# Every fourth weight tile's low part from an accumulating DMA instead of a VectorE subtraction

## The chip, the cores and the metric

One NeuronCore of a Trainium2 chip runs the whole program in one launch. The metric is device time in microseconds, the median of several runs. TensorE (PE in the profile, with PEld for its weight loads) makes the matrix products, VectorE (DVE), ScalarE (ACT) and GpSimd (POOL) work elementwise, and SyncE (SP) issues loads from memory. GpSimd and ScalarE can issue DMAs too. All DMAs run on the same sixteen DMA engines.

## What is computed

Two transformer blocks over 256 tokens of width 2048, batch 1, in float32. Cut to what matters here:

```python
def first_block(x, meta_tokens, ...):          # 16 meta tokens go ahead of the 256
    proj = rmsnorm(h, norm1_w) @ w_in            # 2048 x 4112
    ...                                          # gated linear attention, causal pooling
    h = h + mixed @ w_out                        # 2048 x 2048
    z = rmsnorm(h, norm2_w) @ mlp_w1             # 2048 x 8192
    h = h + jnp.square(jax.nn.relu(z)) @ mlp_w2  # 8192 x 2048
    return rmsnorm(h, final_norm_w)[:, N_META:]

def second_block(x, mem, ...):
    x = layer_norm(ALPHA * x + hybrid_mixer(x, ...), ...)            # w_in 2048 x 9552, w_out
    x = layer_norm(ALPHA * x + mem_cross_attention(x, mem, ...), ...)
    x = layer_norm(ALPHA * x + swiglu(x, w_ffn_in, w_ffn_out), ...)  # 2048 x 11264, 5632 x 2048
    return x
```

What costs time is the products of 256 (or 272) activations with some 450 MB of float32 weights, each of which is used once.

## The kernel before

**Weights as two parts.** TensorE multiplies in float32r, a rounded float32. To keep the accuracy each operand x is held as hi + lo: hi is x rounded to float32r, lo is x - hi. A product is then the sum of three: hi by hi, hi by lo and lo by hi. Activations are split where they are made; weights are split tile by tile as they come in.

**The stream of tiles.** All weights lie in memory in the order of use, cut into 870 tiles of mostly 128 partitions x 1024 float32 (512 KB; two blocks of 128 rows, 512 columns). The class `Stream` holds them. For tile s, `fill` issues the load from SP into a buffer `wraw` (line 51; three buffers, `RAW`), then on ScalarE the rounding copy to `whi` (line 63) and on VectorE the subtraction `wlo = wraw - whi` (line 64; four buffers each, `SPLIT`). `fill` is called by `next`, each time that the program takes a tile for its products. It issues the split of tiles up to two ahead of the one that is taken, and loads up to three ahead of the split. So `whi` and `wlo` of tile s take the buffers of tile s - 4, and `wraw` the buffer of an earlier tile whose split is done. Each engine runs its instructions in the order in which the program issued them, and waits by semaphores for those of other engines.

**The products.** A `TJob` makes out[feature, token] with the weights stationary: for each of four column blocks and two row blocks, a product of `wlo` with the activations' hi part (line 256, 256 columns) and one of `whi` with both parts (line 257, 512 columns). An `NJob` makes out[token, feature] with the activations stationary: three products a step (lines 273 to 275; 274 reads `wlo`). PSUM has six banks `acc` for these. Between products, `side.pump()` issues other work in small steps: evacuations, norms, attention. Of that, some goes to GpSimd: the power function of the norms (`power`, line 377), half of the LayerNorm's scaling in `Turn.prep` (line 469), and DMA loads of row vectors and of the memory tokens (`load`, line 183).

**Order.** The schedule is manual: the order of the program text is the order on each engine. Only the buffer that a new tile gets is chosen for it: of a tag's buffers the pool gives the one that it reckons free first.

Of the kernel before, what the change touches and what calls it, by code (L numbers as in the profile page):

```python
# [11 lines left out]
F32 = mybir.dt.float32  # L12
F32R = mybir.dt.float32r
I32 = mybir.dt.int32
AF = mybir.ActivationFunctionType
# [17 lines left out]
class Stream:  # L33
    """Weight tiles in the order in which the products use them: loaded ahead, and split
    into two float32r parts (hi + lo == w exactly)."""
# [7 lines left out]
    def fill(self, ahead=LOOK):  # L43
        n = len(self.specs)
        nc = self.nc
        while True:
# [11 lines left out]
            if self.s < min(n, self.i + min(ahead, 1 + self.i // 5), self.d):  # L58
# [5 lines left out]
                nc.vector.tensor_tensor(lo, t, hi.bitcast(F32), op=OP.subtract)  # L64
# [21 lines left out]
class Side:  # L86
    """Work that is issued in small pieces between the products of the main sequence.
    Lanes 0 and 1 have a PSUM bank each; lane 2 is for work that needs none."""
# [11 lines left out]
    def post(self, gen):  # L100
        """A chain of steps on one result; one step at a time, chains in order."""
        if isinstance(gen, GeneratorType) and next(gen, self) is not self:
            self.posts.append(gen)
# [38 lines left out]
def wtile(name, kbs, pieces):  # L142
    """One weight tile: rows of the blocks kbs (consecutive), columns of pieces."""
# [9 lines left out]
def hybrid_two_block_kernel(ctx: ExitStack, tc: tile.TileContext, a, out):  # L153
# [40 lines left out]
    def early(d):  # L194
        """Loads between those of the first weights."""
# [23 lines left out]
    prog = []  # L219

    class TJob:
        """out[feature, token]: weights stationary. blocks: (first column, width) in the tile."""
# [39 lines left out]
    class NJob:  # L262
        """out[token, feature]: activations stationary, weights moving."""
# [13 lines left out]
        def run(self):  # L277
# [23 lines left out]
            # the last steps, of one group: the first token tile as a whole before the second  # L301
# [16 lines left out]
    class Call:  # L318
        """fn at this place of the sequence; what is pending is issued first."""
# [31 lines left out]
    def join(dst, b, scale=None, rb=None):  # L351
        """dst = scale * (both halves of the bank) * rb, in two steps"""
# [34 lines left out]
    def square_scale(st, eps, name):  # L387
        """Per token 1 / (mean square + eps), along the partitions."""
# [12 lines left out]
    def row_scale(get, name, parts=((0, 128), (128, 128))):  # L401
        """Per token 1 / rms, along the partitions and along the free axis in all partitions.
        get: the mean square + eps of a part."""
# [19 lines left out]
    def turn_raw(XT, i, g):  # L423
        """Rows of the residual times a weight per feature to XT[feature, block, hi/lo, token]."""
# [16 lines left out]
    class Turn:  # L441
        """LayerNorm of the residual, in place without ln_g and ln_b, and with both to XT."""
# [49 lines left out]
        def spread(self):  # L492
            """As side work."""
# [369 lines left out]
    XT = {}  # L863
# [793 lines left out]
```

## Time and profile before

| | |
|---|---|
| median of 3 runs | 2547.06 us (2547.0 to 2547.12) |
| span of the profiled execution | 2543.4 us |
| TensorE busy | 2520.1 us, 99% |
| VectorE busy | 1611.4 us, 63% |
| ScalarE busy | 1190.8 us, 47% |
| GpSimd busy | 60.6 us, 2% |
| weight tiles | 870, one per 2.92 us of the span |
| DMA | 472.93 MB, mean 186 GB/s |

The profile is one execution; its span runs from the first instruction to the last. Busy time counts an engine's instructions, without waits and without the issuing of DMAs. A group of instructions is named by line, engine, operation and out<-in with the buffers' names; "idle before" is the time in which its engine stood still just ahead of these instructions, and the name behind it is what ended most of that.

### The profile page before, as it was taken

To read this page: it belongs to the slowest core of one execution; us is meant where nothing else is said; L and a number is where in the kernel's file an instruction comes from. 1 tells how busy PE (TensorE), PEld (TensorE's weight loads), DVE (VectorE), ACT (ScalarE), POOL (GpSimd) and SP (SyncE) were. 2 spreads that over 40 slices of the span, in tenths; PEclk is the share of its full clock that TensorE was granted. 3 is DMA by queue.
4 is the path that set the end of the run, shared out by engine and by line. 5 is a ranking of instruction groups with operands and counts; after the bars stand their busy time and mean duration, and the time that the engine had idled before them with its cause. 6 is when DMAs were issued, how large, how long until landed. Compare 5 with 4: busy or idle time off the path is not lost.

```text
span 2543.4 us, 34921 instructions
## 1 busy us (share of the span) xinstructions
PE 2520.1 (99%) x13581; PEld 2160.9 (85%) x13581; DVE 1611.4 (63%) x2240; ACT 1190.8 (47%) x1680; POOL 60.6 (2%) x82
## 2 busy tenths in 40 slices
PE   8999999999999999999999999999999999999998
PEld 8897888888888888888888888888788888888886
DVE  5655666556656656768656667767775555565557
ACT  5444444444444444444544565555544444444443
POOL 0000000000000000000000000020200000000000
PEclk9999999999999999999999999999999999999999
DMA  8444555555566565555555555665566666566664
GB/s 278 133 160 147 164 190 189 191 191 191 183 198 197 190 193 190 187 168 181 172 174 166 166 185 188 224 218 165 190 190 190 193 189 195 186 197 189 193 193 156
DMA packets 132326, 472.93 MB, mean 186 GB/s; under 512 B 14992, under 2 KB 16352, under 8 KB 131888
## 3 DMA queue, kind: packets, MB, share of 16 engines
q1 hardware_dynamic: 128624, 460.77, 56.5%
q0 software_dynamic: 3104, 9.32, 1.3%
q8 instruction: 106, 1.74, 0.3%
q10 hardware_dynamic: 432, 0.61, 0.1%
q14 instruction: 60, 0.49, 0.1%
HBM read 468.54 MB, written 2.10 MB: 185 GB/s over the span
## 4 chain that ended last, share of the span: by engine, by line
PE 96%; DVE 2%; DMA 1%; ACT 1%; issue 0%; POOL 0%; SPq 0%; DVEq 0%; ACTq 0%; POOLq 0%
PE acc L257 34%; PE acc L256 17%; PE acc L273 11%; PE acc L274 11%; PE acc L275 11%; PE acc L253 2%; PE acc L247 2%; PE acc L249 2%; PE acc L248 2%; DMA wraw<-in_weights_dram 1%; PE acc L254 1%; DVE wlo L64 1%; PE aux L1160 0%; PE aux L1090 0%; ACT whi L63 0%
## 5 line engine op out<-in xcount | busy, mean ns | idle before, releaser
L64 DVE TENSOR_TENSOR wlo<-wraw,whi 128x1024 fp32r<-128x1024 f32 (+1 forms) x870 | 1055.6, 1219 | 856.0 <-ACT whi L63 854.6
L63 ACT CAST whi<-wraw 128x1024 fp32r<-128x1024 f32 (+1 forms) x870 | 905.8, 1047 | 1060.4 <-PE acc L257 507.7
L257 PE MATMUL acc<-x5t,whi 128*128 128x512 f32 x1320 | 462.8, 394 | 1.0 <-DVE x5t L490 1.0
L256 PE MATMUL acc<-x5t,wlo 128*128 128x256 f32 x1320 | 366.7, 278 | 0.0
L257 PE MATMUL acc<-x3t,whi 128*128 128x512 f32 x960 | 339.4, 395 | 0.0
L257 PE MATMUL acc<-x2t,whi 128*128 128x512 f32 x960 | 335.9, 394 | 0.0
L257 PEld LDWEIGHTS acc<-x5t,whi 128*128 128x128 f32 x1320 | 247.8, 188 | 54.7 <-DVE x5t L490 1.4
L256 PE MATMUL acc<-x3t,wlo 128*128 128x256 f32 x960 | 272.0, 283 | 0.0
L256 PE MATMUL acc<-x2t,wlo 128*128 128x256 f32 x960 | 266.1, 277 | 0.0
L256 PEld LDWEIGHTS acc<-x5t,wlo 128*128 128x128 f32 x1320 | 248.1, 188 | 4.3 <-DVE wlo L64 0.2
L257 PEld LDWEIGHTS acc<-x2t,whi 128*128 128x128 f32 x960 | 180.0, 187 | 39.0
L257 PEld LDWEIGHTS acc<-x3t,whi 128*128 128x128 f32 x960 | 180.1, 188 | 38.6
L273 PE MATMUL acc<-whi,hid 128*128 128x512 f32 x512 | 199.5, 390 | 0.0
L274 PE MATMUL acc<-wlo,hid 128*128 128x512 f32 x512 | 199.2, 389 | 0.0
L275 PE MATMUL acc<-whi,hid 128*128 128x512 f32 x512 | 199.2, 389 | 0.0
L256 PEld LDWEIGHTS acc<-x3t,wlo 128*128 128x128 f32 x960 | 181.0, 189 | 3.2
L256 PEld LDWEIGHTS acc<-x2t,wlo 128*128 128x128 f32 x960 | 180.2, 188 | 2.9
L274 PE MATMUL acc<-wlo,fh 128*128 128x512 f32 x352 | 137.1, 389 | 0.5 <-DVE wlo L64 0.5
L273 PE MATMUL acc<-whi,fh 128*128 128x512 f32 x352 | 137.0, 389 | 0.0
L275 PE MATMUL acc<-whi,fh 128*128 128x512 f32 x352 | 136.9, 389 | 0.0
L275 PEld LDWEIGHTS acc<-whi,hid 128*128 128x128 f32 x512 | 96.1, 188 | 20.0
L274 PEld LDWEIGHTS acc<-wlo,hid 128*128 128x128 f32 x512 | 96.1, 188 | 19.9
(481 smaller groups left out, 3577.5 us busy)
## 6 DMA issues: line engine op xcount, KB each, us to landing
wraw<-in_weights_dram SPq DMA_DIRECT2D x859, 512.0 KB, 3.6
row<-in_ln_g_dram POOLq DMA_DIRECT2D x12, 256.0 KB, 6.5
wraw<-in_weights_dram SPq DMA_DIRECT2D x8, 336.0 KB, 2.9
ht<-in_hT_dram SPq DMA_DIRECT2D x8, 272.0 KB, 5.1
res<-in_x_dram SPq DMA_DIRECT2D x2, 1024.0 KB, 8.6
row<-in_ln_b_dram POOLq DMA_DIRECT2D x8, 256.0 KB, 9.3
out_dram<-res SPq DMA_DIRECT2D x6, 256.0 KB, 2.7
pw<-in_pool_w_dram SPq DMA_DIRECT2D x1, 1024.0 KB, 8.7
```

What stands on the lines that cost most here:

```text
L63: nc.scalar.copy(hi, t)
L64: nc.vector.tensor_tensor(lo, t, hi.bitcast(F32), op=OP.subtract)
L247: mm(b[:m, :n], wh, x[:, 0], start=first, stop=False)
L248: mm(b[:m, :n], wh, x[:, 1], start=False, stop=False)
L249: mm(b[:m, :n], wl, x[:, 0], start=False, stop=last)
L253: mm(bv, wh, x, start=True, stop=False, skip_group_check=True)
L254: mm(bv[:, 1], wl, x[:, 0], start=False, stop=False, skip_group_check=True)
L256: mm(bv[:, 1], wl, x[:, 0], start=False, stop=False, skip_group_check=True)
L257: mm(bv, wh, x, start=False, stop=last, skip_group_check=True)
L273: mm(b, xh, hi[:, j, :n], start=first, stop=False)
L274: mm(b, xh, lo[:, j, :n], start=False, stop=False)
L275: mm(b, xl, hi[:, j, :n], start=False, stop=last)
```

## The change

```diff
                 nc.scalar.copy(hi, t)
-                nc.vector.tensor_tensor(lo, t, hi.bitcast(F32), op=OP.subtract)
+                if self.s >= 16 and self.s % 4 == 0:
+                    nc.scalar.activation(lo, t, AF.Copy, scale=-1.0)
+                    nc.gpsimd.dma_start(lo, t, accum_op=OP.add)
+                else:
+                    nc.vector.tensor_tensor(lo, t, hi.bitcast(F32), op=OP.subtract)
```

For the tiles s = 16, 20, 24, ... 868, 214 of 870, ScalarE writes the negated rounded tile to `wlo`, by a second pass over `wraw` with the factor -1. Then a DMA issued by GpSimd adds `wraw` to `wlo` in place, from SBUF to SBUF: wlo = -hi + w. The other tiles are as before. Everything else in the diff removes comments; lines after 64 have numbers larger by four.

What this does to the order of instructions is shown at three places. In `wraw_3980` and the like the number counts tiles as they are allotted; "waits" lists the semaphores, where DMAHW stands for DMAs issued by SP or ScalarE, DMASW for those issued by GpSimd, and Activation, DVE, PE and Pool for the engines.

SP's queue, loads of tiles 135 to 141, in the down projection of the first feed-forward. Before:

```order
L51 DMA wraw_3911<-in_weights_dram 128x1024 [waits DMAHW0_49,DVE_49]
L51 DMA wraw_3950<-in_weights_dram 128x1024 [waits DMAHW1_49,DVE_49]
L51 DMA wraw_3977<-in_weights_dram 128x1024 [waits DMAHW2_49,DVE_49]
L51 DMA wraw_3995<-in_weights_dram 128x1024 [waits DMAHW3_49,DVE_49]
L51 DMA wraw_4013<-in_weights_dram 128x1024 [waits DMAHW4_49,DVE_49]
L51 DMA wraw_4033<-in_weights_dram 128x1024 [waits DMAHW5_49,DVE_49]
L51 DMA wraw_4053<-in_weights_dram 128x1024 [waits DMAHW6_49,DVE_49]
```

and with the change:

```order
L51 DMA wraw_3941<-in_weights_dram 128x1024 [waits DMAHW0_49,DMASW2_49,Activation_49]
L51 DMA wraw_3980<-in_weights_dram 128x1024 [waits DMAHW1_49,DVE_49]
L51 DMA wraw_4007<-in_weights_dram 128x1024 [waits DMAHW2_49,DVE_49]
L51 DMA wraw_4025<-in_weights_dram 128x1024 [waits DMAHW3_49,DVE_49]
L51 DMA wraw_4044<-in_weights_dram 128x1024 [waits DMAHW5_49,DVE_49]
L51 DMA wraw_4064<-in_weights_dram 128x1024 [waits DMAHW4_49,DMASW3_49]
L51 DMA wraw_4084<-in_weights_dram 128x1024 [waits DMAHW6_49,DVE_49]
```

Tile 132 and tile 136 (`wraw_3980`) are changed ones. Before, each load waits for VectorE, which has subtracted from the tile that the buffer held. Now the load of tile 135 (`wraw_3941`) waits for a DMA of GpSimd, the accumulate of tile 132, and that of tile 140 (`wraw_4064`) for the accumulate of tile 136, whose buffer it takes; tile 139 takes that of tile 137. Counted over the queue, 87 of the accumulates are waited for by the load three tiles on, 123 by the load four tiles on, and 3 by one five or six tiles on.

ScalarE, casts of tiles 134 to 138. Before:

```order
L63 CAST whi_3973<-wraw_3889 128x1024 [waits DMAHW2_49,PE_49,Activation_49]
L63 CAST whi_3991<-wraw_3911 128x1024 [waits DMAHW3_49,PE_49,Activation_49]
L63 CAST whi_4009<-wraw_3950 128x1024 [waits DMAHW4_49,PE_49,Activation_49]
L63 CAST whi_4029<-wraw_3977 128x1024 [waits DMAHW5_49,PE_49,Activation_49]
L63 CAST whi_4049<-wraw_3995 128x1024 [waits DMAHW6_49,DVE_49,PE_49]
```

and with the change:

```order
L63 CAST whi_4003<-wraw_3918 128x1024 [waits DMAHW2_49,PE_49,Activation_49]
L63 CAST whi_4021<-wraw_3941 128x1024 [waits DMAHW3_49,PE_49,Activation_49]
L63 CAST whi_4039<-wraw_3980 128x1024 [waits DMAHW4_49,PE_49,Activation_49]
L65 ACTIVATE wlo_4040<-wraw_3980 128x1024 [waits DMASW2_49]
L63 CAST whi_4060<-wraw_4007 128x1024 [waits DMAHW5_49,PE_49,Activation_49]
L63 CAST whi_4080<-wraw_4025 128x1024 [waits DMAHW6_49,DVE_49,PE_49]
```

Behind the cast of tile 136 stands its second pass, into `wlo_4040`, ahead of the cast of tile 137. It waits for nothing but the last DMA into that buffer.

GpSimd's queue, at the LayerNorm after the mixer of the second block. Before:

```order
L377 TENSOR_TENSOR lr_14850<-lv_14849,mhalf_80 128x2 [waits DVE_49]
L469 TENSOR_SCALAR res_73<-res_73,mw_14848,lr_14850 128x256 [waits DMAHW6_49,Pool_49]
L469 TENSOR_SCALAR res_73<-res_73,mw_14848,lr_14850 128x256 x5
L183 DMA row_15132<-in_ln_g_2_dram 128x512 [waits DMAHW1_49,DMASW5_49,PE_49]
L183 DMA row_15133<-in_ln_b_2_dram 128x512 [waits DMAHW0_49,DMASW6_49,DMAHW4_49,PE_49,Activation_49]
L183 DMA row_15132<-in_ln_g_2_dram 128x512 [waits DMASW7_49]
```

and with the change:

```order
L66 DMA wlo_14963<-wraw_14912 128x1024 [waits DMASW1_49,DMASW0_49,DMAHW4_49,PE_49,Activation_49]
L381 TENSOR_TENSOR lr_14991<-lv_14990,mhalf_80 128x2 [waits DVE_49]
L473 TENSOR_SCALAR res_73<-res_73,mw_14989,lr_14991 128x256 [waits DMAHW6_49,Pool_49]
L473 TENSOR_SCALAR res_73<-res_73,mw_14989,lr_14991 128x256 x5
L66 DMA wlo_15085<-wraw_14997 128x1024 [waits DMASW2_49,DMASW1_49,DMAHW0_49,PE_49,Activation_49]
L66 DMA wlo_15231<-wraw_15126 128x1024 [waits DMASW2_49,DMAHW4_49,PE_49,Activation_49]
L187 DMA row_15275<-in_ln_g_2_dram 128x512 [waits DMAHW1_49]
L187 DMA row_15276<-in_ln_b_2_dram 128x512
L66 DMA wlo_15369<-wraw_15281 128x1024 [waits DMASW3_49,DMAHW0_49,PE_49,Activation_49]
```

The accumulates (`wlo_...`) stand between the LayerNorm's power and scaling and the loads of rows, each waiting for its load, for ScalarE's pass and for TensorE, which read the buffer before; what stands behind them on GpSimd waits with them. VectorE's queue only loses the 214 subtractions.

## Rows read from the trace of the kernel before

**Rows 1.** The page's part 1: engine, busy us (share of the span), instructions.
```profile
span 2543.4 us, 34921 instructions
PE 2520.1 (99%) x13581; PEld 2160.9 (85%) x13581; DVE 1611.4 (63%) x2240; ACT 1190.8 (47%) x1680; POOL 60.6 (2%) x82
```

**Rows 2.** The page's part 4: the chain that ended last, by engine and by line.
```profile
PE 96%; DVE 2%; DMA 1%; ACT 1%; issue 0%; POOL 0%; SPq 0%; DVEq 0%; ACTq 0%; POOLq 0%
PE acc L257 34%; PE acc L256 17%; PE acc L273 11%; PE acc L274 11%; PE acc L275 11%; PE acc L253 2%; PE acc L247 2%; PE acc L249 2%; PE acc L248 2%; DMA wraw<-in_weights_dram 1%; PE acc L254 1%; DVE wlo L64 1%; PE aux L1160 0%; PE aux L1090 0%; ACT whi L63 0%
```

**Rows 3.** TensorE's waits: engine, line, waited for: us in total, times, longest us.
```profile
PE acc L247 <- ACT whi L63: 5.6, 1, 5.6
...
PE acc L249 <- DVE wlo L64: 0.7, 1, 0.7
...
PE acc L274 <- DVE wlo L64: 0.5, 1, 0.5
```

**Rows 4.** The page's part 5: count, busy us, mean ns, idle before, releaser.
```profile
L64 DVE TENSOR_TENSOR wlo<-wraw,whi 128x1024 fp32r<-128x1024 f32 (+1 forms) x870 | 1055.6, 1219 | 856.0 <-ACT whi L63 854.6
L63 ACT CAST whi<-wraw 128x1024 fp32r<-128x1024 f32 (+1 forms) x870 | 905.8, 1047 | 1060.4 <-PE acc L257 507.7
```

**Rows 5.** Timeline of ScalarE, then VectorE, quiet stretch: start us, us, instruction [idle before].
```profile
2002.98 1.05 ACT L63 CAST whi<-wraw 128x1024 fp32r<-128x1024 f32 x1 [1.66 <-PE acc L275]
2005.70 1.05 ACT L63 CAST whi<-wraw 128x1024 fp32r<-128x1024 f32 x1 [1.67 <-PE acc L275]
...
2004.07 1.22 DVE L64 TENSOR_TENSOR wlo<-wraw,whi 128x1024 fp32r<-128x1024 f32 x1 [1.50 <-ACT whi L63]
```

**Rows 6.** The raw tiles from 2000 to 2100 us: time from issue to landing.
```profile
L51 SPq DMA_DIRECT2D wraw<-in_weights_dram x37: 327/328/328, 1999.9 to 2099.3; - x37
...
DMA to landing us min/median/max: 3.3/3.5/4.6
```

**Rows 7.** Line 64 alone by stretch: us, DVE busy (count), clock, DMA share, GB/s.
```profile
300.00:1100.00 800.00, 351.25 (x292) 1.00 0.59 191
1500.00:1700.00 200.00, 87.90 (x73) 1.00 0.63 202
1800.00:2500.00 700.00, 308.38 (x253) 1.00 0.62 195
100.00:300.00 200.00, 70.55 (x58) 1.00 0.48 154
1100.00:1500.00 400.00, 158.50 (x130) 1.00 0.55 170
1700.00:1800.00 100.00, 33.53 (x29) 0.98 0.52 169
```

**Rows 8.** DMA queues (packets, MB, share of engines); issues (count, KB, us to landing).
```profile
q1 hardware_dynamic: 128624, 460.77, 56.5%
q0 software_dynamic: 3104, 9.32, 1.3%
...
pb<-in_k_dist_dram POOLq DMA_DIRECT2D x1, 192.0 KB, 2.6
```

**Rows 9.** The rows loaded by GpSimd: durations in ns min/median/max, and landing.
```profile
L183 POOL DMA_DIRECT2D row<-in_ln_g_dram x12: 536/550/629, 1703.9 to 2472.1; - x12
...
DMA to landing us min/median/max: 4.0/6.8/12.2
```

**Rows 10.** Timeline of GpSimd: start us, us, instruction, count.
```profile
1608.60 2.12 POOL L183 DMA_DIRECT2D mem<-in_memT_dram  x4 [534.67 <-DVE ev L1287]
...
1693.63 10.34 POOL L469 TENSOR_SCALAR res<-res,mw,lr 128x256 f32<-128x256 f32 x6
1703.92 0.63 POOL L183 DMA_DIRECT2D row<-in_ln_g_dram  x1
...
1791.86 10.05 POOL L469 TENSOR_SCALAR res<-res,mw,lr 128x256 f32<-128x256 f32 x6
```

**Rows 11.** All engines by stretch: us, busy (count) of PE, PEld, DVE, ACT, POOL; clock.
```profile
1789.00:1791.00 2.00, 0.48 (x2) 0.14 (x1) 1.75 (x5) 1.09 (x2) 0.11 (x1) 1.00 0.01 4
1791.00:1793.00 2.00, 0.55 (x3) 0.31 (x3) 1.17 (x4) 0.37 (x1) 1.69 (x2) 1.00 0.00 0
1793.00:1795.00 2.00, 1.14 (x7) 0.93 (x8) 1.23 (x4) 1.86 (x5) 2.00 (x3) 0.85 0.00 0
1795.00:1797.00 2.00, 2.00 (x8) 1.81 (x7) 1.33 (x3) 1.48 (x3) 2.00 (x3) 0.50 0.00 0
1797.00:1799.00 2.00, 2.00 (x11) 1.73 (x11) 1.87 (x4) 1.99 (x3) 2.00 (x2) 0.79 0.00 0
```

## Prediction

> **What bounds the kernel now.** I read the busy table first: TensorE works 2520.1 us of a span of 2543.4, VectorE 1611.4, ScalarE 1190.8, GpSimd 60.6 [rows 1]. The chain of work that ended last is TensorE for 96%, the subtraction at line 64 for 1% [rows 2]. So the kernel is bound by TensorE's products, and VectorE, from which the change takes work, is not waited for: in all waits of TensorE the subtraction ends 0.7 and 0.5 us [rows 3]. Whatever the change frees on VectorE has about nothing to win; what it can lose is decided by whether a weight tile's low part is still ready when TensorE comes to it.
>
> For that I read the feeding of tiles. Each of 870 tiles is cast by ScalarE (whi, 1047 ns mean) and subtracted by VectorE (wlo, 1219 ns) [rows 4]. In a quiet stretch casts start 2.72 us apart, each released by TensorE, which frees the parts of the tile four places earlier; the subtraction starts 0.04 us after the cast ends [rows 5]. So tile s is split in 2.3 us while TensorE still has three tiles, 3 x 2.72 = 8.2 us, ahead of it: 5.9 us of slack. The raw tile is free when the split ends; its slot's next load takes 3.5 us from issue to landing (3.3 to 4.6) [rows 6], against the 8.2 us after which it is wanted.
>
> The pace of tiles sets what a group of four has. Counting line 64 by stretch: 292 + 73 + 253 = 618 tiles in 1700 us (dense, 2.75 us a tile, 11.0 a group), and 58 + 130 + 29 = 217 in 700 us where other products lie between (loose, 3.23, 12.9 a group) [rows 7]. That is 154 dense and 54 loose groups; the rest are at the start and the end.
>
> **The change, part by part.** 214 tiles (s = 16, 20, ... 868) are changed.
> Removed: 214 subtractions of 1.22 us, 261 us of VectorE. Off the path, by the waits above: worth 0.
> Added on ScalarE: 214 passes of the shape of the cast. The trace has no such pass with a scale; the cast's 1.05 us [rows 4] is its nearest row: 225 us, on an engine that is free for half the time. Hidden as far as ScalarE's time goes; as latency it stands between cast and DMA.
> Added on GpSimd: 214 DMA issues of some 0.55 us (those of the row loads [rows 9]): 118 us on an idle engine.
> Added as transfer: each DMA takes in the raw tile and the old low part, 512 KB each, and writes 512 KB. The trace has no accumulating DMA and no transfer inside SBUF, so I bound its time A, from issue to landing. From below: a plain load of the same bytes, 3.5 us [rows 6]. From above: the longest of the row loads, 12.2 us for 256 KB in a burst of eight [rows 9]. For a middle value: the load queue keeps the sixteen DMA engines 56.5% busy for 460.77 MB [rows 8], so 524,288 bytes take 0.565 x 2543.4 x 0.524/460.77 = 1.64 us of all sixteen; the other 1.9 of the 3.5 us is fixed. On GpSimd's queue the 192 KB load took 2.6 us [rows 8], of which 0.6 is bytes by the same rate, so 2.0 is fixed there. With two streams to read, A = 2.0 + 2 x 1.64 = 5.3 us if nothing shares the engines, and 5.3 + 1.6 = 6.9 beside one weight load. With the write counted as a third pass it is 6.9 and 8.5. I take the two-pass value, since the load too writes what it reads and its 1.64 us holds both sides.
> The Trainium skill, "Collectives: The Full Stack", section on the bandwidth ceiling, says that a reduce runs at half the rate of a copy because the add needs two source reads on one ring; by it the bytes count twice, A is 5.3 and 6.9 us and the time 2845 us; by the plain load's row it is 3.5 us and at most 2567. The rule speaks against the change, and no row of this trace can show it.
>
> Where this lies on the path: within the tile first. The split now takes 1.05 + 0.04 + 1.05 and 0.1 for the hand-over to GpSimd, 2.25 us before the issue, then A: 2.25 + 5.3 = 7.6 us of the 8.2 there are. A single tile is just in time. But the raw tile is held until the DMA has landed, and loads wait for it. The order of SP's queue shows which: after 87 of the accumulates the load three tiles on waits for it, after 123 the load four tiles on, which is the next changed tile itself (the pool gives out the slot that it reckons free first). Behind that load stand all later loads on SP. So the accumulates form a loop:
> - four on (123 groups): issue 2.25 after the cast's start, A beside one weight load 6.9, hand-over to SP 0.1, load 3.5: 12.75 us;
> - three on (87): 2.25 + 5.3 + 0.1 + 3.5, and 1.64 for the second load, which brings the changed tile: 12.8 us.
> Both are longer than the 11.0 us that TensorE needs for four dense tiles, by 1.8 us, and about as long as the 12.9 of a loose group. Sum: 154 x 1.8 = 277 us; loose groups 0.
> GpSimd's queue: an accumulate stands behind what GpSimd does. At 1693.6 and 1791.9 us it has 10 us of TENSOR_SCALAR, then eight row loads of 256 KB each, and at 1608.6 us eight memory loads [rows 10]. In the new order accumulates follow these; with 0.6 us of slack in a tile, each of the three places costs up to its delay, some 7 us: 20 us, or 0 where TensorE waits there anyway (it is busy 0.48 and 0.55 of two stretches of 2 us near 1790 [rows 11]).
> Behind a delayed cast ScalarE's copies out of PSUM wait too; TensorE has six banks, and in a kernel paced by tiles these copies have the same time to spare. Taken at 0; in the worst case it is inside the range.
> Total: 277 + 20 = +297 us on the profiled 2543.4; the median 2547.06 is 3.7 us above that span. 2547 + 297 = 2844, say 2845 us.
>
> **Rivals.**
> (a) The transfer is hidden. If A is 3.5 us as for a plain load, the loops are 9.35 and 10.99 us, both within 11.0, and only GpSimd's bursts are left: 2547 to 2567 us; not slower in the first case. It decides where the loops reach 11.0 us: A = 3.5 (three on) and 5.1 (four on), 4.4 in the mean of both. For it: GpSimd's queue moves its bytes nearly as fast as SP's (1.3% of the engines' time for 9.32 MB, 56.5% for 460.77 [rows 8]: 0.14 and 0.12 a MB). Against: two streams instead of one, and row loads that take 4.0 us at least for half the bytes [rows 9].
> The Trainium skill, "DMA: Bandwidth & Descriptors", section "Anatomy of one DMA — SWDGE (gpsimd) path", fits a plain GpSimd DMA by 2.0 us and the bytes at 436 GB/s; for 512 KB that is an estimate of 3.2 us, which would land here.
> (b) It is hidden and VectorE's relief pays: the subtraction's 1% of the chain lies where VectorE is crowded; a quarter of it gone is 6 us: 2541 us.
> (c) The DMA is dearer: a third pass or a slower add, A of 6.9 and 8.5: loops of 14.35, 3.35 us over in 154 groups and 1.45 in 54: 516 + 78 + 20 = +614, 3160 us. With A = 9.3 throughout (between this and the 12.2 row) it is 15.2: 4.2 x 154 + 2.3 x 54 + 20 = +790, 3340. TensorE's gaps of 3 us and more might also lower its clock: after it had idled from 1789 to 1793 us, the granted clock was 0.85, 0.50 and 0.79 in the next three stretches of 2 us [rows 11]. That is paid out of the gap itself as long as the loop is the longer of the two.
> (d) Not all 214 tiles go this way: the order shows 214 DMAs and 214 passes; no chance.
>
> **How the numbers follow.** The loop with two passes, 2600 to 3050 us: 0.60. (a) 0.14, of which 0.06 is within 0.2% (5 us, about what a measurement of this kernel can tell from no change). (b) 0.02. (c) 0.24. So faster 0.02, same 0.06, slower 0.92. The range takes the likeliest case whole, the edge of (a) from 2565 (0.04 of its 0.14), and of (c) 0.16 of 0.24, up to 3300 (A of about 9.2); outside lie 0.12 below and 0.08 above.
>
> **What would show it.** Right: TensorE's busy share falls to some 88%, with gaps once in four tiles, ended by the accumulating DMA on the low part's weight loads or products; SP waits for the DMA into wlo; casts wait for raw loads; the DMA into wlo lands after 5 to 7 us; accumulates lie 12.8 us apart. Wrong: a landing time of under 4 us with no wait of TensorE for it (a), or over 8 (c). The sum is wrong in its structure if the DMA takes 5 to 7 us and accumulates still follow each 11 us.

## The result: 2742.8 us against 2547.1, slower by 7.7%

The changed kernel took 2742.75 us (median of 4 runs, 2738.05 to 2744.52), the kernel before beside it 2547.09 (2547.0 to 2547.29): a ratio of 1.0769, 95% interval 1.0756 to 1.0782, or +196 us. The forecast was 2845 (+298), range 2565 to 3300. The sign and the mechanism came out, the size was two thirds. The profiled execution has a span of 2739.8 us.

The page of the changed kernel: the busy table, two queues, the three groups that the change touches, and the two kinds of DMA (the columns are those of [rows 1, 4, 8]).

```profile
PE 2588.1 (94%) x13581; PEld 2181.3 (80%) x13581; DVE 1372.2 (50%) x2026; ACT 1380.1 (50%) x1894; POOL 244.1 (9%) x296
...
q1 hardware_dynamic: 128624, 460.77, 49.0%
q0 software_dynamic: 33920, 121.17, 24.2%
...
L63 ACT CAST whi<-wraw 128x1024 fp32r<-128x1024 f32 (+1 forms) x870 | 908.1, 1045 | 1121.8 <-DMA wraw<-in_weights_dram 811.2
...
L66 POOL DMA_DIRECT2D wlo<-wraw x214 | 183.4, 857 | 2427.9 <-ACT wlo L65 1511.6
...
L65 ACT ACTIVATE wlo<-wraw 128x1024 fp32r<-128x1024 f32 x214 | 225.0, 1051 | 0.0
...
wraw<-in_weights_dram SPq DMA_DIRECT2D x859, 512.0 KB, 4.2
wlo<-wraw POOLq DMA_DIRECT2D x212, 512.0 KB, 4.9
```

VectorE lost 239 us of work [rows 1] and nobody gained by it. ScalarE's new pass costs 1051 ns, as the cast does [rows 4]. The accumulating DMA lands 4.9 us after its issue begins; the 0.86 us that GpSimd needs to issue it lie inside that time. TensorE is idle 151.7 us (span less busy) in place of 23.3 [rows 1], and its busy time is 68 us longer. By an estimate (0.9% of 2588 us) the granted clock, 0.988 in place of 0.997, makes up 24 of these 68; what the others are is not shown here.

Waits of TensorE, of SP's queue and of ScalarE in the changed kernel (engine, line, waited for: us in total, times, longest us), each the longest of its engine:

```profile
PE acc L260 <- DMA wlo<-wraw: 65.3, 54, 4.2
PE acc L278 <- DMA wlo<-wraw: 45.2, 37, 3.4
...
SPq L51 <- DVE wlo L68: 1044.4, 421, 15.7
SPq L51 <- DMA wlo<-wraw: 940.4, 212, 10.9
...
ACT whi L63 <- DMA wraw<-in_weights_dram: 811.2, 398, 8.2
```

TensorE now waits for the accumulating DMA, 110.5 us in two lines where the subtraction ended 1.2 us before [rows 3]. The rows of SP and ScalarE say why that DMA is late: SP, which loads the weights, waits 212 times for an accumulate to land, and ScalarE waits 811 us for raw tiles, which in the kernel before came to 137.6 us. Of the 214 changed tiles, 156 had their cast held up by the raw load, and on these 156 fall 100 of the 110.5 us. After 212 of the accumulates a load goes out within 0.5 us of the landing.

One turn of the loop, in a dense stretch of the changed kernel (ScalarE, GpSimd and SP's issues; start us, us; behind the issues the time from issue to landing of that one):

```profile
2411.11 1.05 ACT L63 CAST whi<-wraw 128x1024 fp32r<-128x1024 f32 x1 [1.28 <-DMA wraw<-in_weights_dram]
2412.06 1.05 ACT L65 ACTIVATE wlo<-wraw 128x1024 fp32r<-128x1024 f32 x1
2413.41 0.86 POOL L66 DMA_DIRECT2D wlo<-wraw  x1 [11.85 <-ACT ev L350]
DMA to landing us min/median/max: 4.5/4.5/4.5
2418.01 0.33 SPq L51 DMA_DIRECT2D wraw<-in_weights_dram  x1
2418.43 0.38 SPq L51 DMA_DIRECT2D wraw<-in_weights_dram  x1
DMA to landing us min/median/max: 4.5/4.5/4.5
2421.77 1.05 ACT L63 CAST whi<-wraw 128x1024 fp32r<-128x1024 f32 x1 [1.25 <-DMA wraw<-in_weights_dram]
2423.03 1.05 ACT L63 CAST whi<-wraw 128x1024 fp32r<-128x1024 f32 x1 [0.20 <-DMA wraw<-in_weights_dram]
2425.33 0.86 POOL L66 DMA_DIRECT2D wlo<-wraw  x1 [11.06 <-ACT wlo L65]
```

From cast to cast: 2.30 to the issue, 4.5 to the landing (2417.96), 0.05 to the first waiting load, 0.42 to the second, 4.5 until that one, which brings the next changed tile, has landed, 0.1 to its cast: 11.9 us, against the 11.0 that TensorE needs for four tiles [rows 7]. Over the whole kernel GpSimd's timeline has 12.11 us from issue to issue in the dense stretches (mean of 150 groups) and 13.47 in the rest (63 groups, 0.57 more than the 12.9 of [rows 7]): 150 x 1.11 + 63 x 0.57 = 202 us. That this comes near the 196 us seen tells where the time went and not why: whatever makes a tile late lengthens these intervals, ScalarE's second pass too. That the held raw tile is the reason rests on the waits above and on the runs below.

### The profile page after: what moved, and what is told of

The parts are those of the page before. It is cut to its first block, busy times and chain, and to the rows that moved or that the text cites. A ratio compares the mean times of both kernels' runs of the same rounds, so it can differ in the third digit from the quotient of the medians.

```text
span 2739.8 us, 35328 instructions
## 1 busy us (share of the span) xinstructions
PE 2588.1 (94%) x13581; PEld 2181.3 (80%) x13581; DVE 1372.2 (50%) x2026; ACT 1380.1 (50%) x1894; POOL 244.1 (9%) x296
## 3 DMA queue, kind: packets, MB, share of 16 engines
q0 software_dynamic: 33920, 121.17, 24.2%
## 5 line engine op out<-in xcount | busy, mean ns | idle before, releaser
L68 DVE TENSOR_TENSOR wlo<-wraw,whi 128x1024 fp32r<-128x1024 f32 (+2 forms) x656 | 798.4, 1218 | 1063.7 <-ACT whi L63 1062.8
L261 PE MATMUL acc<-x5t,whi 128*128 128x512 f32 x1320 | 474.0, 399 | 0.0
L260 PE MATMUL acc<-x5t,wlo 128*128 128x256 f32 x1320 | 376.4, 285 | 35.0 <-DMA wlo<-wraw 34.1
L66 POOL DMA_DIRECT2D wlo<-wraw x214 | 183.4, 857 | 2427.9 <-ACT wlo L65 1511.6
L65 ACT ACTIVATE wlo<-wraw 128x1024 fp32r<-128x1024 f32 x214 | 225.0, 1051 | 0.0
L260 PEld LDWEIGHTS acc<-x3t,wlo 128*128 128x128 f32 x960 | 181.9, 190 | 16.4 <-DMA wlo<-wraw 13.1
```

What stands on the lines that cost most here:

```text
L65: nc.scalar.activation(lo, t, AF.Copy, scale=-1.0)
L66: nc.gpsimd.dma_start(lo, t, accum_op=OP.add)
L260: mm(bv[:, 1], wl, x[:, 0], start=False, stop=False, skip_group_check=True)
L261: mm(bv, wh, x, start=False, stop=last, skip_group_check=True)
```

## The experiments

Twelve more kernels ran, each four times beside the kernel before (medians of 2546.4 to 2547.8 us). In the table: the accumulating (or copying) DMA from its issue to its landing, median; TensorE's waits for it; ScalarE's waits for raw loads; and a quiet stretch, from the first to the last of the 352 products `acc<-wlo,fh` (197 tiles, 550.3 us in the kernel before, so 11.2 us for four).

| kernel | us | ratio (95%) | landing | TensorE for it | casts for raw loads | quiet stretch |
|---|---|---|---|---|---|---|
| changed | 2742.8 | 1.0756-1.0782 | 4.9 | 110.5 | 811 | 598.3 |
| e1 every fifth | 2692.4 | 1.0541-1.0593 | 4.9 | 79.9 | 612 | 583.6 |
| e2 source in device memory | 2879.7 | 1.1269-1.1352 | 6.9 | 220.4 | 74 | 636.5 |
| e3 plain copy | 2597.6 | 1.0179-1.0213 | 3.1 | 20.9 | 583 | 557.8 |
| e4 the pass only | 2571.7 | 1.0077-1.0107 | - | - | 175 | 553.1 |
| e5 source the high part | 2790.6 | 1.0912-1.1025 | 6.3 | 158.3 | 92 | 619.8 |
| e6 negated pass first | 2853.2 | 1.1179-1.1226 | 6.0 | 174.4 | 976 | 631.6 |
| e7 every eighth | 2633.7 | 1.0323-1.0354 | 5.0 | 35.7 | 508 | 559.1 |
| e8 every third | 2856.5 | 1.1196-1.1246 | 4.8 | 175.2 | 899 | 624.7 |
| e9 half a tile | 2712.5 | 1.0641-1.0677 | 3.8 | 52.1 | 737 | 591.4 |
| e10 copy of the high part | 2640.8 | 1.0350-1.0402 | 5.5 | 55.4 | 181 | 577.6 |
| e11 half loads | 2621.0 | 1.0272-1.0320 | 5.5 | 32.5 | 41 | 559.7 |
| e12 hold only | 2854.4 | 1.1163-1.1229 | (two copies) | 0 | 989 | 641.6 |

### What the parts cost: e4, e3, e2

e4 keeps ScalarE's second pass and lets VectorE subtract all tiles.

```diff
-                    nc.gpsimd.dma_start(lo, t, accum_op=OP.add)
-                else:
-                    nc.vector.tensor_tensor(lo, t, hi.bitcast(F32), op=OP.subtract)
+                nc.vector.tensor_tensor(lo, t, hi.bitcast(F32), op=OP.subtract)
```

> Only ScalarE's second pass is added for every fourth tile; VectorE then subtracts over it as before, and there is no accumulate. Theory, the loop, and both rivals on the DMA: the pass is hidden and makes the split 1 us longer within 5.9 us of slack: 2547 to 2552 us. Rival, ScalarE: if its pass delays casts and evacuations, a good part of the 196 us shows here: above 2600 us.

It took 2571.73 us: 24 us for what was booked at nothing. This is the price of the pass together with a subtraction behind it, which waits for the pass here and which the changed kernel doesn't have; the pass by itself was not run. I matched TensorE's 13,581 instructions, which stand in the same order in both kernels, one by one: between the two profiled executions 12.9 of 27 us are lost from 1700 to 1820 us of the kernel before, where the rows of the residual are normalised. TensorE's longest waits of e4 there, and, over the whole of e4, VectorE's waits for the pass:

```profile
PE aux L477 <- DVE res L471: 4.7, 2, 2.7
PE aux L477 <- DVE l1a L487: 2.3, 2, 2.0
PE aux L525 <- ACT res L469: 1.9, 1, 1.9
...
DVE wlo L66 <- ACT wlo L65: 329.8, 176, 4.3
```

In the kernel before ScalarE is busy for 15.6 and VectorE for 16.4 of the 20 us from 1700 to 1720, so an engine that is half free on average has little to spare there. The two longest of these waits are for VectorE.

e3 copies the raw tile into the low part and adds nothing.

```diff
-                    nc.gpsimd.dma_start(lo, t, accum_op=OP.add)
+                    nc.gpsimd.dma_start(lo, t)
```

> The DMA copies the raw tile over the low part instead of adding to it (the low part is then the whole weight: this part of the computation is changed); all waits and holds stay. Theory, the loop: only the landing time changes, from 4.9 us to that of one stream, about 3.5; the loops are 2.3 + 3.5 + 4.4 = 10.2 us (load four on) and 11.7 (three on) against 11.0: 2550 to 2600 us. Rival, sharing: the engines still move two thirds of the bytes, so about two thirds of the loss: 2680 us. If the landing time stays at 4.9 us, a second stream costs nothing and the time stays at 2740 us.

2597.6 us, just inside the loop theory's range and 82 below the number of sharing. GpSimd's queue and the copy's landing in e3:

```profile
q0 software_dynamic: 33920, 121.17, 13.5%
...
DMA to landing us min/median/max: 2.4/3.1/6.1
```

The copy lands after 3.1 us where the accumulate takes 4.9, and takes 13.5% of the DMA engines in place of 24.2%. Without the row loads (1.3% of 2543.4 us [rows 8]) that is 1.48 us of all sixteen engines a copy and 2.94 an accumulate. So the adding is worth 1.8 us of landing and 145 of the 196 us; copy and pass together cost 51, of which e4's 24 may be the pass.

e2 lets the accumulate read the weights a second time from device memory, so that the raw tile is not held (cut: the lines that keep each load's source in `self.w`).

```diff
-                    nc.gpsimd.dma_start(lo, t, accum_op=OP.add)
+                    nc.gpsimd.dma_start(lo, self.w[self.s], accum_op=OP.add)
```

> The accumulate reads the weight tile from memory again instead of from the raw buffer, so the raw buffer is free after ScalarE's second pass and no load waits for an accumulate; tiles, passes, DMA count and result stay. Theory, the loop: without the held buffer there is none, and a changed tile has 2.3 + about 5 of its 8.2 us: 2547 to 2580 us, with 0.5 MB more read for each changed tile. Rival, lateness within the tile: the DMA takes as long or longer, so 2740 us or more. Rival, sharing of the DMA engines: the same transfers and more from memory, so 2740 us or more.

2879.7 us, as both rivals had it. The hold is gone (casts wait 74 us for raw loads), but the DMA now lands after 6.9 us, so this run did not isolate the hold. From the cast to the landing are 9.3 us (median), and TensorE gives a tile some 8.1 (worked out with e7 below): 213 of 214 tiles are over, 284 us in sum. With e4's 24 that is 308 of the 332 us lost. So lateness inside the tile can cost as much as the hold.

### How often: e1, e7, e8

These change `% 4` to `% 5`, `% 8` and `% 3` and nothing else.

> Every fifth tile (s = 20, 25, ..., 170 of them) is changed instead of every fourth. Theory, the loop: the accumulate holds the raw buffer, the loads behind it on SP wait, and one accumulate follows the other after some 12.1 us (mean between issues in the dense stretches of the changed kernel). Five dense tiles give TensorE 13.75 us, so the loop is the shorter one: 2547 to 2575 us. Rivals: if each changed tile is late by itself (2.3 us to the issue and 4.9 to the landing, of 8.2 us), or if the added transfers slow the weight loads by sharing the DMA engines, the price goes with the number of changed tiles: 2547 + 196 x 170/214 = about 2703 us.

2692.4 us, near the number of the rivals. Here the budget is 13.75 us, and a turn read like the one above came to 14.9: behind the landing the second load took 5.7 us, the accumulate 5.5, and GpSimd started 0.8 us late. Other turns show another way that my forecast lacked: only 25 of the 170 changed tiles wait for their own raw load, but in 128 turns that cast or one of the two ahead of it does, and ScalarE, which works in order, passes the delay on. So a budget longer by one tile did not clear the effect of the hold.

> 107 changed tiles in place of 214, 22.0 us apart in the dense stretches in place of 11.0. Hold theory: the loads have caught up before the next changed tile (loop of 14 us at most against 22), so only the pass (half of 24 us) and the spread of the landing (0.2 to 0.35 us in 107 tiles, 20 to 40 us) are left: 2565 to 2600 us. Rival, a fixed cost of each changed tile, 0.92 us as in the changed kernel: 2547 + 107 x 0.92 = 2645 us (2635 to 2655).

2633.7 us, outside my range and just below the rival's. Both are right in a place. In the quiet stretch 24 tiles cost 8.8 us, 0.37 each, where the changed kernel paid 48.0 for 50, 0.96 each: with 22 us between them the loads do catch up. In the crowded stretches (320 to 1180 and 1450 to 1940 us of the kernel before) e7 lost 38 and 37 us, as much for each tile as the changed kernel (65 and 70 for twice as many). There 18 of 60 accumulates land after 6.2 us or more, 12 of these 18 with two weight loads beside them; in the quiet stretch it is 3 of 24. Two tiles of e7, the accumulate's landing and TensorE's wait behind it; a third one with 4.6 us had none either:

```profile
L66 POOL DMA_DIRECT2D wlo<-wraw x1: 850/850/850, 451.5 to 451.5; - x1
DMA to landing us min/median/max: 7.0/7.0/7.0
PE acc L278 <- DMA wlo<-wraw: 1.5, 1, 1.5
...
L66 POOL DMA_DIRECT2D wlo<-wraw x1: 850/850/850, 474.6 to 474.6; - x1
DMA to landing us min/median/max: 4.7/4.7/4.7
```

Tile by tile (320 to 1000 and 2000 to 2300 us), a landing of up to 5.5 us cost under 0.2 us but for two tiles whose raw load was late, and one of 6.2 or more cost 0.7 to 2.3. So a tile bears some 5.6 to 5.8 us of landing behind its 2.3 us, 8.1 us in all, when its cast is not late.

> 284 changed tiles in place of 214, 8.25 us apart in the dense stretches, and after most of them the load of the very next changed tile waits for the accumulate. Loop theory: 8.06 us to the landing, 0.1 to SP, a load of 4.2 to 4.7 us: some 12.6 us a loop against 8.25 dense (206 loops) and 9.7 loose (72): 206 x 4.35 + 72 x 2.9 = 1105 us more, 3650 us (3450 to 3800). Rival, a fixed cost of each changed tile: 2547 + 284 x 0.92 = 2808 us (2790 to 2830).

2856.5 us, far from 3650 and nearer to the rival's 2808, though above its range too. Two things in my expectations for e5 to e8 were wrong. The landing is counted from the start of the issue, so their "0.86 + 4.9" counts the issue twice, and the tile's way is 2.3 + 4.9 = 7.2 us, not 8.06. And for e8 I took the wrong load: 209 of its 284 accumulates are waited for by the load four tiles on, which is the one behind the next changed tile. The loop then spans two groups, in a turn that I read: landing, that load (5.1), its cast and subtraction (2.3), the load into the slot which these free (3.8), cast of a changed tile, 2.3 and 4.7 to its landing, with hand-overs 18.5 us for two. GpSimd's timeline has 9.19 us from issue to issue (median) against 8.25 for three tiles.

The price of a changed tile is 0.80 us in e7, 0.85 in e1, 0.91 in the changed kernel and 1.09 in e8: a fixed price would have forecast the totals better than my loop did. What tells the causes apart is where TensorE waits. Count from a changed tile's cast to the time at which TensorE has nothing left but that tile's low part; in the kernel before this would be some 8.2 us. Of the waits for accumulates, 103 of 110 us (changed kernel), 74 of 80 (e1) and 170 of 175 (e8) come where it is under 7.5 us, so where the cast was late. In e7 these are 24 of 36 us, and in e5, the next run, 25 of 158.

### Without the hold: e5, e10, e11

e5 is the changed kernel with another source of the same bytes; the raw tile is free after ScalarE's pass.

```diff
-                    nc.gpsimd.dma_start(lo, t, accum_op=OP.add)
+                    nc.gpsimd.dma_start(lo, hi.bitcast(F32), accum_op=OP.add)
```

> Same 214 tiles, same pass, same accumulating DMA of the same bytes between SBUF and SBUF, but it reads the cast high part in place of the raw tile (the low parts of these tiles come out as zero, so that part of the computation is left out). The path inside the tile stays 0.95 + 1.05 + 0.30 + 0.86 + 4.9 = 8.06 us of 8.25; the raw tile is free after ScalarE's second pass, 2.0 us after the cast's start in place of 8.06. Hold theory (a changed tile has no slack left, and its cast comes late because its raw load waited for an earlier accumulate): casts wait for raw loads about as in the kernel before (137.6 us in all, against 811.2 in the changed kernel), SP waits for no accumulate, and what is left is the pass alone, 2572, plus the spread of the accumulate's landing (0.2 to 0.35 us in 214 tiles, 40 to 75 us): 2575 to 2645 us. Rival, lateness inside the tile alone, and rival, transfers that share the DMA engines: nothing of either changes, 2720 to 2745 us.

2790.6 us, slower than the changed kernel: the theory that the hold is the cause by itself fell here. The hold did go (SP waits for no accumulate), but the landing went from 4.9 to 6.3 us. Waits and landing of e5:

```profile
PE acc L260 <- DMA wlo<-whi: 103.5, 80, 4.9
PE acc L278 <- DMA wlo<-whi: 54.4, 50, 3.9
...
ACT whi L63 <- DMA wraw<-in_weights_dram: 92.4, 48, 6.6
...
DMA to landing us min/median/max: 4.5/6.3/9.9
```

One changed tile of e5 (SP's issue, GpSimd's, the accumulate's landing, TensorE's wait) shows where that came from:

```profile
2401.58 1.05 ACT L63 CAST whi<-wraw 128x1024 fp32r<-128x1024 f32 x1 [3.71 <-PE acc L261]
2402.53 1.06 ACT L65 ACTIVATE wlo<-wraw 128x1024 fp32r<-128x1024 f32 x1
2403.62 0.33 SPq L51 DMA_DIRECT2D wraw<-in_weights_dram  x1
2403.88 0.86 POOL L66 DMA_DIRECT2D wlo<-whi  x1 [12.17 <-ACT ev L350]
DMA to landing us min/median/max: 6.7/6.7/6.7
2410.64 0.38 PE L260 MATMUL acc<-x5t,wlo 128*128 128x256 f32 x1 [0.74 <-DMA wlo<-whi]
```

The end of ScalarE's pass frees the raw tile and starts the accumulate, so a weight load goes out 0.26 us before this accumulate, as before nearly all of them, and runs beside it. With about one load beside it the accumulate took 6.3 us (145 tiles), with about two 7.5 (68). In the changed kernel the hold keeps back the loads that need the held slot: 4.8 us where a load ran for less than half of the accumulate (87 tiles), 5.2 where for more (127); in 112 of these it is one for another slot, which goes out some 1.9 us after the accumulate's issue. From cast to landing e5 has 8.6 us (median), over 8.1 in 212 of 214 tiles, 196 us in sum, plus e4's 24: 220 of 243.

e11 keeps e5's accumulate and halves the loads beside it (cut: the cast, the pass and the subtraction in two halves each, and e5's source).

```diff
-                nc.sync.dma_start(t, bass.AP(tensor=self.src.tensor, offset=self.src.offset + self.at,
-                                             ap=[[kq * cols, 128], [cols, kq], [1, cols]]))
+                w = cols // 2 if self.d >= 16 else cols
+                nc.sync.dma_start(t[:, :, :w], bass.AP(tensor=self.src.tensor, offset=self.src.offset + self.at,
+                                                       ap=[[kq * cols, 128], [cols, kq], [1, w]]))
```

> Accumulate from the high part as in the run at 2790.6 us (raw tile not held), but from tile 16 on each weight load brings half its columns, which the cast, the pass and the subtraction read twice, in two instructions each (so the products are of other weights, and the low parts of the 214 tiles are zero). The accumulate keeps its bytes. Sharing theory (A grows beside weight loads because they use the same DMA engines): a half load takes 0.77 of the engines in place of 1.53 us, A falls from 6.3 to some 5.0 to 5.5 and is again inside 5.8 less the 0.2 us that the two halves of cast and pass add: 2570 to 2620 us. Rival, A is 6.3 us because it reads what ScalarE has just written, or because of its engine's own pace, whatever loads beside it: A stays over 6.0 and the time over 2740 us.

2621.0 us: the landing fell from 6.3 to 5.5 and the time by 170 us, 1 us above the upper edge of what sharing gave, and far from the rival's 2740. The accumulate and its bytes are the same, so at least these 0.8 us of its landing in e5 came from the loads' bytes. (The half loads also land sooner, after 3.1 us against 4.3, so the 170 us need not all be the accumulate's. Cast and pass as two instructions each add some 0.2 us to the tile's way, so neither are the 75 us that are left.)

e10 is e3 with e5's source.

> The accumulating DMA becomes a plain copy and reads the cast high part, so the raw tile is not held (the low parts of 214 tiles come out as copies of the high parts; that part of the computation is changed). Two-cause theory: A is 3.1 alone and about 4.6 beside loads, under 5.8, and nothing is held: only the pass is left, 2565 to 2585 us; the plain copy from the raw tile took 2597.6, so the hold alone was worth some 25 us there. Rival, every transfer beside the loads costs by its share of the DMA engines: the same bytes as in the plain copy, 2595 to 2605 us.

2640.8 us, neither number: slower than e3 by 43, by the same exchange. The step that failed is "about 4.6 beside loads": with a load going out at the same moment each time the copy took 5.3 us, with two 6.4, median 5.5 against e3's 3.1.

### The hold alone: e12

VectorE makes all low parts, and at the 214 tiles two copies to device memory hold the raw tile.

```diff
+                nc.vector.tensor_tensor(lo, t, hi.bitcast(F32), op=OP.subtract)
                 if self.s >= 16 and self.s % 4 == 0:
-                    nc.scalar.activation(lo, t, AF.Copy, scale=-1.0)
-                    nc.gpsimd.dma_start(lo, t, accum_op=OP.add)
-                else:
-                    nc.vector.tensor_tensor(lo, t, hi.bitcast(F32), op=OP.subtract)
+                    mark = self.pool.tile([128, 1], F32, name="mark", tag="mark", bufs=1)
+                    nc.gpsimd.tensor_copy(mark, lo.bitcast(F32)[:, 0, 0:1])
+                    for c in range(2):
+                        at = (2 * (self.s // 4 % 8) + c) * 131072
+                        nc.gpsimd.dma_start(bass.AP(tensor=self.scratch.tensor, offset=self.scratch.offset + at,
+                                                    ap=[[kq * cols, 128], [cols, kq], [1, cols]]), t)
```

> All low parts are made by VectorE as in the kernel before, ScalarE has no second pass, and no product waits for a GpSimd DMA. At the 214 tiles GpSimd reads one column of the finished low part and then copies the raw tile twice to a scratch in device memory, so that the raw tile is held for some 2.3 us of cast and subtraction, 0.5 us to the issue and 4 to 5 us to the second landing, about as long as in the changed kernel, with about as many bytes moved beside the loads. Hold theory: the chain from a held tile's cast over its copies' landing to the next loads and the next held tile's cast is 2.3 + 0.5 + 4 to 5 + 0.1 + 4.0 to 4.9 = 11 to 12.8 us against 11.0 to 11.2, although every low part is made 5.9 us before it is wanted: casts wait for raw loads for hundreds of us, and the time is 2600 to 2740 us, with TensorE waiting for VectorE's low parts and ScalarE's high parts. Rival, only lateness inside the changed tile counts (the accumulate's own landing): nothing is late here, 2547 to 2565 us. If the second landing comes under 3.8 us after the issue the chain fits and the run does not decide.

2854.4 us, more than the hold theory gave and 300 from the rival. Waits of TensorE, then of ScalarE and SP, in e12:

```profile
PE acc L261 <- DVE ev L368: 60.9, 17, 8.0
PE acc L261 <- DVE sg L368: 41.3, 9, 7.3
PE acc L264 <- DVE wlo L65: 19.5, 27, 2.4
PE acc L282 <- DVE wlo L65: 14.4, 18, 1.9
...
ACT whi L64 <- DMA wraw<-in_weights_dram: 989.2, 486, 8.0
...
SPq L52 <- DMA scratch<-wraw: 540.1, 196, 8.3
```

No product waits for a DMA here and each split is the fast one, yet the casts wait 989 us for raw loads. Behind them on ScalarE stand the copies out of PSUM, and behind these the steps of VectorE (`ev`, `sg`) for which TensorE then waits longest. The raw tile is held for 8.2 us from its cast (median), one more than in the changed kernel, and the groups follow each other after 12.7 us (median). Slower loads are not the reason. The landing of a load in e12, then in e5, whose casts wait only 92 us:

```profile
DMA to landing us min/median/max: 2.8/4.3/9.9
...
DMA to landing us min/median/max: 2.1/4.3/9.4
```

So the hold is shown to pace the kernel by itself, however much slack a low part has. The total is not the changed kernel's price of it: the hold is longer, 224 MB more are written to device memory, and the granted clock was 0.967.

### Two ways to shorten the way: e6, e9

e6 makes the negated pass before the cast; e9 gives the DMA half the columns and VectorE the other half.

```diff
                 if self.s >= 16 and self.s % 4 == 0:
                     nc.scalar.activation(lo, t, AF.Copy, scale=-1.0)
                     nc.gpsimd.dma_start(lo, t, accum_op=OP.add)
+                    nc.scalar.copy(hi, t)
                 else:
+                    nc.scalar.copy(hi, t)
```

> In the 214 tiles ScalarE makes the negated pass first and the cast after it, so the accumulate starts 1.05 us sooner: 0.95 + 0.30 + 0.86 + 4.9 = 7.0 us of 8.25 inside the tile, and the raw tile is free 1.05 us sooner. Latency theory (with or without the hold): each dense period falls by up to 1.05 us, 12.11 to 11.1, and the loose ones lose what they had over, 150 x 1.0 + 30 = 180 us less than 2743: 2565 to 2610 us. Rival, sharing of the DMA engines: the same bytes at the same rate, 2725 to 2745 us.

2853.2 us, a loss of 110 where I expected a gain of 150. The issue does come 0.95 us sooner (1.36 us after the pass's start), but two things moved. The pool now gives the slot so that after 203 accumulates (87 in the changed kernel) it is the load three tiles on that waits, and three loads go out in a burst (139 turns; 28 in the changed kernel); and the accumulate starts while the third of them is under way and lands after 6.0 us. The 110 us are not split between the two. The loop is 1.4 + 6.0 + 0.5 + 4.5 + 0.1 = 12.5; measured 12.66 (median).

```diff
+                    h = cols // 2
                     nc.scalar.activation(lo, t, AF.Copy, scale=-1.0)
-                    nc.gpsimd.dma_start(lo, t, accum_op=OP.add)
+                    nc.gpsimd.dma_start(lo[:, :, :h], t[:, :, :h], accum_op=OP.add)
+                    nc.vector.tensor_tensor(lo[:, :, h:], t[:, :, h:], hi.bitcast(F32)[:, :, h:], op=OP.subtract)
```

> The same 214 tiles, the same pass and as many accumulating DMAs, but each takes in half the columns (256 KB); VectorE subtracts the other half. New theory, after the runs above: a changed tile is late by two causes that both come from the bytes of its DMA: (1) from its cast's start to the landing there are 2.3 us and A (counted from the start of the issue; the 0.86 us of the issue lie inside it), which may be 8.1 us together, so A up to 5.8; A is 4.8 alone and 6.2 to 7.5 beside more than one weight load; (2) the raw tile is held until the landing, so the loads behind it are late, loop 2.33 + A + 0.5 + 4.4 against 11.0. With half the bytes A is 1.9 + 2.94/2 = 3.4 alone and up to 5 beside loads: inside 5.8, and the loop is 10.6: both causes are gone but for the spread, as with the plain copy (A 3.4): 2572 for the pass and up to 30 more: 2570 to 2605 us. Rival, a fixed price for each accumulating DMA: 2725 to 2745 us; half and half: 2660.

2712.5 us: closer to the rival's number than to mine, for another reason. With 3.8 us of landing TensorE waits for the DMA only 52 us, and the way in the tile is over 8.1 us in only two tiles, so the first cause is gone; but 206 accumulates now hold the load three tiles on, with bursts of three in 117 turns: 2.35 + 3.8 + 0.5 + 4.5 + 0.1 = 11.3 in such a turn, 11.94 measured (median). My 10.6 took the slots as they are in the changed kernel. The 0.6 us between turn and median, and how much of the 166 us a fixed price of the DMA might be, stay open.

## Why the prediction was right, and where it was off

**What bounds, and VectorE's relief.** Right: TensorE, and 239 us off VectorE bought nothing. Rival (b) is out. The signs named are there, each smaller than forecast: TensorE busy 94% (88), gaps ended by the accumulate, SP and the casts waiting, landing after 4.9 us (5 to 7), accumulates 12.1 us apart (12.8).

**A, the time to landing.** The two-stream reckoning gave 5.3 alone and 6.9 beside a load. Measured: 4.8 where little of a load runs beside it, 4.9 in the median, and 6.2 to 6.3 when a load starts with it (e5). The engines' time, 2.94 us against 1.48 for the copy, is the two passes that were assumed. The Trainium skill, "Collectives: The Full Stack", "The bandwidth ceiling: the fold count and why AG ≠ RS ≠ AR", has a reduce of a collective at half the copy's rate because of two source reads: 2.94 against 1.48 us of the engines' time agrees for this local add. The Trainium skill, "DMA: Bandwidth & Descriptors", "Anatomy of one DMA — SWDGE (gpsimd) path", fits a plain GpSimd DMA by 2.0 us and the bytes at 436 GB/s, an estimate of 3.2 us for 512 KB: e3's copy, 3.1, agrees. For the accumulate, at 4.9, that is the wrong price.

**In the tile: just in time.** 2.25 + 5.3 = 7.6 of 8.2 was forecast; 2.30 + 4.9 = 7.2 was measured. Over 8.1 us were 29 of 214 tiles, 9 us in sum. So in the changed kernel the tile's own way costs almost nothing by itself, as reckoned; it costs where the cast is late already.

**The loop.** This is the term of the sum that was mis-sized. The split of the slots was right, 87 and 123 in the trace too. For three on, 12.8 was forecast and 12.2 (median) to 12.6 (mean) measured. For four on, 12.75 was forecast and 11.65 to 11.8 measured: the step "A beside one weight load 6.9" failed, because a load runs beside only a part of the accumulate: the one that needs the held slot goes out after the landing, the one ahead of it mostly 1.9 us after the accumulate's issue (0.6 of a load ran beside it on average, and A's mean is 5.1). So 154 x 1.8 = 277 became 150 x 1.11 = 166 us, with the share of ScalarE's pass inside. The load's 3.5 us was too short: 4.2 in the median, 4.4 as the second of two; that took back part of the first error. That the total came out at two thirds is in part luck: the dense groups were set 111 us too high, the loose groups and the pass too low.

**Loose groups at 0.** They cost 36 us, again with the pass inside. I take the reason to be that their budget of 12.9 is a mean, and that what a long group has over does not help a short one; no run shows it.

**ScalarE's pass at 0.** In e4 it is 24 us, with the subtraction behind it, the clearest miss: half of it in a stretch of 120 us where the average over the span said nothing. In the changed kernel it lies inside the 166 and 36 us and does not come on top.

**GpSimd's bursts, 20 us.** The delay did not come. In the changed kernel the row and memory loads mostly go out behind accumulates, and of the accumulates near the three places one is issued 3.4 us and one 3.1 us after its cast began, the others after 2.3. The first of these two, with what GpSimd did before it and with its cast and pass:

```profile
1799.45 7.96 POOL L473 TENSOR_SCALAR res<-res,mw,lr 128x256 f32<-128x256 f32 x5
...
1803.98 1.05 ACT L63 CAST whi<-wraw 128x1024 fp32r<-128x1024 f32 x1 [0.99 <-DMA wraw<-in_weights_dram]
1804.94 1.06 ACT L65 ACTIVATE wlo<-wraw 128x1024 fp32r<-128x1024 f32 x1
...
1807.36 0.88 POOL L66 DMA_DIRECT2D wlo<-wraw  x1
```

So GpSimd's queue delayed an accumulate by 1.1 us where 7 were forecast. The stretch from 1700 to 1820 us lost 20.5 us, but e4 without any DMA lost 12.9 there.

**Rivals.** (a) would have needed A of 3.5; e3 shows it: with 3.1 and a hold, 2598 us, 31 above the 2567 that (a) gave, and e4's 24 may be the pass. (c) did not come: A never was 6.9 in the changed kernel. What I had not listed is how the two causes trade: free the raw tile sooner and the loads run beside the accumulate, which then is late in its own tile (e5, e10); keep it, and the loads are late (e12).

## What to carry to other kernels

A transfer that takes the place of a short engine step does not only have to land in time: it holds what it reads until then, so reckon the whole turn (source ready, transfer, next load into the freed buffer, next use) against the pace of the consumer, and do it with the load's time beside other loads. Before freeing a buffer sooner or starting a transfer earlier, ask what will then run beside it; here both made it worse, by 48 and 110 us (the second with the loads in other slots too). And a pass put on an engine that is half idle is priced stretch by stretch, with what waits behind it, and not by the engine's average.

## What the runs showed of the hardware that was not expected

- An accumulating DMA of 512 KB inside SBUF landed after 4.9 us (3.8 to 6.7), a plain copy after 3.1 (2.4 to 6.1), an accumulate from device memory after 6.9 (5.5 to 9.1). GpSimd took 0.86 us to issue either accumulate and 0.53 to issue the copy.
- Half the columns of each row (256 KB in pieces of half the length) still landed only after 3.8 us, and the issue took 1.19 us, longer than for the whole tile; the queue shows 61312 packets in place of 33920.
- TensorE's granted clock was 0.997 in the kernel before, 0.988 in the changed one and 0.967 in e12, where TensorE was busy 92% of the span; e8, also at 92%, had 0.979.
